# First expert matrix: both parts of the input side by side in one 512-column stream, and the one-hots of the first key on ScalarE

## The chip, the cores and the metric

The kernel runs on 1 NeuronCore of one Trainium2 chip. The metric is the device time of one execution in microseconds (us). The numbers before are three timed executions and one profiled execution of the same program.

## The reference

A hybrid layer on 256 tokens of width 2048 (16 more tokens stand ahead in its first part): retention and state-space mixing, then a product-key expert layer with 128 x 128 experts, then a last norm. What the change touches is the expert layer, for all 256 tokens at once:

```
xn   = rmsnorm(h, norm_ffn_g)                       # 256 x 2048, fp32
q    = (xn @ w_q).reshape(tokens, 8, 2, 128)        # 8 heads, two half keys
s    = einsum('thcd,hckd->thck', q, sub_keys)       # two scores of 128 keys
s1, i1 = top_k(s[:, :, 0], 16);  s2, i2 = top_k(s[:, :, 1], 16)
cand = s1[..., :, None] + s2[..., None, :]          # 256 candidates, top 16 again
eid  = i1 * 128 + i2 of the 16 chosen;  gate = softmax(top_s)
act  = gelu(einsum('td,thkd->thk', xn, exp_u[eid]))
out  = einsum('thk,thkd->td', gate * act, exp_v[eid])
```

The kernel does not gather rows. It multiplies xn by all 16384 rows of exp_u, takes the gelu, weights it by a 128 x 128 table of gates for each token, which is zero where an expert was not chosen, and multiplies by all of exp_v.

## The kernel before, in words

All weights come as 512 KB blocks of 128 x 1024 through one queue of SP (`Stream.load`, L90). A block is two *pieces* of 128 x 512. For each piece ScalarE copies the raw fp32 weights to the fp32r tile `wh` (L100), VectorE subtracts to get the rest `wl` (L101), and TensorE multiplies in three terms: high by high, low by high, high by low. The list of pieces is the program's clock: `Stream.run` goes from piece to piece, splits the piece two ahead, lets the side work that is due issue its instructions, and then issues the piece's matmuls. All orders are fixed when the program is built, and each engine works in that order.

Side work is written as generators. `yield wait, dve, act` asks for a rest of so many pieces and announces so much work on VectorE and ScalarE. `Stream.due` gives each piece a credit of 0.70 on VectorE and 0.80 on ScalarE (`SPARE`). Work that isn't urgent is put off by a piece when a credit that it wants is not above zero; a debt is carried into the next piece.

The expert layer has these stages, in the order of the pieces. In the first the input is h times the weights of the norm, not yet divided by its root mean square: `Q.xgh` and `Q.xgl`, 16 chunks of 128 x 256 each (`scaled`, L819 and L822). The reciprocal root, spread over a tile of 128 x 256, is `Q.rb` (`norm`, L835).

- Queries: 16 products of 4 pieces (`query`). From `norm` on the side work `topk` picks the keys on VectorE, some 146 pieces' worth of its credit, into `Q.i1`, `Q.i2` and the gates.
- First expert matrix ("the U stage"): 128 units of 4 pieces (`product`, L207 to L209, with 16 chunks of three matmuls of 256 columns each). After a unit VectorE multiplies the sums by `Q.rb` (L1030), and ScalarE takes the gelu (L1036, and L1038 for tokens whose gates are there already). While units run, the side work `gates` builds the gate table token by token: GpSimd makes the one-hots of the first key (L985), VectorE two weighted ones of the second key (L987), and one matmul of 256 columns makes the table (L1001). Each token asks for 0.26 on VectorE, and at most one token is taken in a piece. After four tokens `into_z` copies one half on ScalarE (L1016, asking for 0.7) and a piece later adds on VectorE (L1021, L1023, asking for 0.7) and multiplies on GpSimd (L1025, L1041). All gates have to be there before the last stage.
- Second expert matrix ("the V stage"): 128 x 4 pieces, matmuls of 512 columns (L1069 to L1071).

SP issues all loads of weights. The table `Q.iota`, which the one-hots are compared with, is loaded when the U stage opens (`u_open`, L961); `u_open` also gives back the memory of `h2p`.

Of the kernel before, what the change touches and what calls it, by code (L numbers as in the profile page):

```python
# [12 lines left out]
OP = mybir.AluOpType  # L13
# [114 lines left out]
def build(ctx, tc, a):  # L128
# [61 lines left out]
    def product(srcs, moving, done, hook=None, count=None):  # L190


        nk = 8 * len(srcs)
        box = {}

        def piece(k0):
            def f(h, lo):
                if count:
                    st.need(lambda: count() >= k0 + 4)
                mh, ml = moving()  # L200
                if k0 == 0:
                    box["p"] = P.psa.tile([128, T], F32, name="acc")
                p = box["p"][:, :mh.shape[-1]]
                for k in range(4):
                    s = slice(k * 128, k * 128 + 128)
                    kk = k0 + k
                    pe.matmul(p, h[:, s], mh[:, kk], start=kk == 0, stop=False)  # L207
                    pe.matmul(p, h[:, s], ml[:, kk], start=False, stop=False)  # L208
                    pe.matmul(p, lo[:, s], mh[:, kk], start=False, stop=kk == nk - 1)  # L209
                if k0 + 4 == nk:  # L210
                    st.spawn(done(p), 1, True)
            return f

        st.queue += [(srcs[i // 2], piece(4 * i), hook if i == 0 else None) for i in range(2 * len(srcs))]
# [568 lines left out]
    def resid_open():  # L783
        closed("gated", "xn")
        w = opened("bconst")
        Q.rb = w.tile([128, S], F32, name="rb")
        w = opened("xg")
        Q.xgh = w.tile([128, NK, S], F32R, name="xgh")
        Q.xgl = w.tile([128, NK, S], F32R, name="xgl")
        w = opened("h2p")  # L790
        Q.h2 = w.tile([128, 2, D], F32, name="h2")
        Q.ss = w.tile([128, 2, 4], F32, name="ss")
        nc.sync.dma_start(Q.h2, a["xt"])
        Q.h2d = P.dram.tile([128, 2, D], F32, name="h2d")
# [31 lines left out]
    def norm():  # L826
        yield 6
        sq = P.bconst.tile([128, 2], F32, name="sq")
        vec.tensor_reduce(sq, Q.ss, axis=AX.X, op=OP.add)
        Q.rt = P.bconst.tile([128, 2], F32, name="rt")  # L830
        rsqrt(Q.rt, sq, 1.0 / D, EPS)
        yield 3
        ps = P.psm.tile([128, 512], F32, name="mix")
        yield from rows(ps[:, :S], Q.rt, P.h2p.tile([128, 512], F32, name="junk")[:, :S])
        act.activation(Q.rb, ps[:, :S], AF.Copy)  # L835
        st.spawn(topk(), 1)

    def query_open():
        closed("mhl", "mwork", "merged")
# [43 lines left out]
    def topk():  # L883
# [53 lines left out]
        for i in range(3):  # L937
# [5 lines left out]
            tps.append(t)  # L943
            yield 1
        Q.i1, Q.i2, g = tps
        gh = P.slots.tile([128, S], F32R, name="gh")
        act.activation(gh, g, AF.Copy)
        vec.tensor_sub(g, g, gh.bitcast(F32))
# [6 lines left out]


    def u_open():
        closed("h2p")
        w = opened("bwork", 2)
        Q.iota = w.tile([128, 128], F32, name="iota", bufs=1)  # L960
        nc.sync.dma_start(Q.iota, a["iota"])  # L961
        opened("slots")
        opened("psg", 2, space=PSUM)
        w = opened("zap")
        Q.za = w.tile([128, NE - ZB, S], F32, name="za")
        Q.nblk = 0
        Q.ntok = 0
# [11 lines left out]
    def gates():  # L979
        NB = 4  # L980

        def hot(t):
            tt = slice(t, t + 1)
            o = P.ohp.tile([128, 3, 128], F32R, name="o", bufs=3)
            pool.tensor_scalar(o[:, 0], Q.iota, Q.i1[:, tt], None, op0=OP.is_equal)  # L985
            for i in range(2):
                vec.tensor_scalar(o[:, 1 + i], Q.iota, Q.i2[:, tt], Q.gg[i][:, tt], op0=OP.is_equal, op1=OP.mult)  # L987
            return o

        os = []  # L990
        for t in range(2):
            yield 1, 0.26
            os.append(hot(t))
        for t in range(S):
            yield 1, 0.26
            if t + 2 < S:
                os.append(hot(t + 2))
            if t % NB == 0:
                ps = P.psg.tile([128, NB, 2, 128], F32, name="g")
            o = os.pop(0)  # L1000
            pe.matmul(ps[:, t % NB].rearrange("p a b -> p (a b)"), o[:, 0], o[:, 1:].rearrange("p a b -> p (a b)"),  # L1001
                      start=True, stop=True)
            if t % NB == NB - 1:
                st.spawn(into_z(ps, t + 1 - NB, t + 1), 1, False, (0, 0.7))
        while Q.ntok < S:
            yield 1
        yield 1
        closed("ohp")
        opened("wp", 2, side="right")
        Q.w = {}  # L1010
        for i in range(2):
            st.spawn(split_w(i), i + 1)
# [14 lines left out]
    def unit(i):  # L1027
        def done(p):
            t = P.bwork.tile([128, S], F32, name="ut", bufs=2)
            vec.tensor_mul(t, p, Q.rb)  # L1030
            yield 1, 0, 0.45
            n = Q.ntok
            Q.nblk = i + 1
# [160 lines left out]
            q = st.queue[-8:]  # L1194
            st.queue[-8:] = q[:2] + q[4:6] + q[2:4] + q[6:]
    for i in range(NE):
        product([a["pu"][i, 0], a["pu"][i, 1]], lambda: (Q.xgh, Q.xgl), unit(i), u_open if i == 0 else None)
    for i in range(NE):
        for q in range(4):
            hook = {(0, 0): v_open, (0, 3): v_open3, (NE - ZB + 3, 0): fin_open}.get((i, q))  # L1200
# [179 lines left out]
```

## Time and profile before

| what | value |
|---|---|
| median of 3 timed runs | 3375.70 us (3375.68 to 3375.73) |
| profiled execution: its time | 3375.47 us |
| profiled execution: span of the core | 3373.7 us |
| TensorE matmul busy | 3352.7 us, 99% |
| VectorE, ScalarE, GpSimd busy | 2339.9, 1742.1, 634.8 us |

The span is what the trace covers; some 1.8 us of the execution's time lie around it. The duration that the trace gives to a matmul runs from its start to its modelled end, and matmuls overlap, so what a matmul costs is read from the spacing of the starts: the number of matmuls in a stretch that has no gap. The same holds for the other engines, where an instruction can begin before the one ahead of it has ended.

### The profile page before, as it was taken

How to read it: one execution, taken by the hardware profiler on the slowest of the kernel's cores; microseconds unless marked ns; L12 is line 12 of the kernel's file. 1: busy time of each engine (PE TensorE's matmuls, PEld its weight loads, DVE VectorE, ACT ScalarE, POOL GpSimd, SP SyncE). 2: the span in 40 equal slices, each digit the busy share in tenths (PEclk: the TensorE clock that was granted, in tenths of full speed). 3: DMA queues.
4: the chain of work that ended last, by engine and by line, in shares of the span. 5: the costliest groups of instructions: out<-in, count | busy, mean ns of one | idle time of the engine just before them, and what ended most of it. 6: DMA issues, size and time to landing. Idle time of an engine off the chain costs nothing.

```text
span 3373.7 us, 60928 instructions
## 1 busy us (share of the span) xinstructions
PE 3352.7 (99%) x22638; PEld 3101.6 (92%) x22638; DVE 2339.9 (69%) x4521; ACT 1742.1 (52%) x3148; POOL 634.8 (19%) x726
## 2 busy tenths in 40 slices
PE   9999999999999999999999999999999999999998
PEld 9999999888899999988889999999999988888886
DVE  7555555555578878865556899899999655555555
ACT  5444444444455555554455555555555555555555
POOL 1100110000023323310000111356778200000000
PEclk9999999999999999999999999999999999999999
DMA  6555555566655555556666565555555666666665
GB/s 202 159 168 164 170 167 164 173 196 205 188 175 177 176 180 182 181 172 189 188 214 211 175 188 186 178 177 176 176 176 176 187 194 193 194 194 194 218 207 162
DMA packets 174249, 619.81 MB, mean 184 GB/s; under 512 B 20320, under 2 KB 22240, under 8 KB 173696
## 3 DMA queue, kind: packets, MB, share of 16 engines
q1 hardware_dynamic: 169728, 602.16, 57.8%
q0 software_dynamic: 3648, 12.72, 1.3%
q8 instruction: 178, 2.92, 0.4%
q14 instruction: 119, 0.97, 0.1%
q10 hardware_dynamic: 576, 1.05, 0.1%
HBM read 611.52 MB, written 4.33 MB: 183 GB/s over the span
## 4 chain that ended last, share of the span: by engine, by line
PE 56%; ACT 0%; DVE 0%; issue 0%; POOL 0%; POOLq 0%; ACTq 0%
PE acc L209 8%; PE acc L208 8%; PE acc L207 8%; PE y L1069 7%; PE y L1070 7%; PE y L1071 7%; PE acc L235 3%; PE acc L236 3%; PE acc L237 3%; PE g L1001 1%; PE mix L469 0%; PE mix L863 0%; DVE wl L101 0%; ACT junk L1122 0%; ACT wh L100 0%
## 5 line engine op out<-in xcount | busy, mean ns | idle before, releaser
L101 DVE TENSOR_TENSOR wl<-raw,wh 128x512 fp32r<-128x512 f32 x2244 | 1631.9, 732 | 977.3 <-ACT wh L100 764.8
L100 ACT ACTIVATE wh<-raw 128x512 fp32r<-128x512 f32 x2244 | 1409.1, 630 | 1299.5 <-PE acc L208 664.6
L207 PE MATMUL acc<-xh,wh 128*128 128x272 f32 (+1 forms) x2640 | 768.3, 291 | 0.0
L209 PE MATMUL acc<-xh,wl 128*128 128x272 f32 (+1 forms) x2640 | 753.7, 286 | 0.6 <-DVE wl L101 0.6
L208 PE MATMUL acc<-xl,wh 128*128 128x272 f32 (+1 forms) x2640 | 751.1, 285 | 0.0
L209 PE MATMUL acc<-xgh,wl 128*128 128x256 f32 x2304 | 644.6, 280 | 0.0
L207 PE MATMUL acc<-xgh,wh 128*128 128x256 f32 x2304 | 643.9, 279 | 0.0
L208 PE MATMUL acc<-xgl,wh 128*128 128x256 f32 x2304 | 643.8, 279 | 0.0
L207 PEld LDWEIGHTS acc<-xh,wh 128*128 128x128 f32 x2640 | 497.5, 188 | 3.9 <-issue 1.2
L209 PEld LDWEIGHTS acc<-xh,wl 128*128 128x128 f32 x2640 | 497.4, 188 | 1.0 <-DVE wl L101 1.0
L208 PEld LDWEIGHTS acc<-xl,wh 128*128 128x128 f32 x2640 | 497.4, 188 | 0.7
L208 PEld LDWEIGHTS acc<-xgl,wh 128*128 128x128 f32 x2304 | 432.8, 188 | 0.1
L209 PEld LDWEIGHTS acc<-xgh,wl 128*128 128x128 f32 x2304 | 432.3, 188 | 0.0
L207 PEld LDWEIGHTS acc<-xgh,wh 128*128 128x128 f32 x2304 | 432.1, 188 | 0.1
L1069 PE MATMUL y<-wh,wzh 128*128 128x512 f32 x1024 | 398.5, 389 | 0.0
L1070 PE MATMUL y<-wl,wzh 128*128 128x512 f32 x1024 | 398.5, 389 | 0.0
L1071 PE MATMUL y<-wh,wzl 128*128 128x512 f32 x1024 | 398.5, 389 | 0.0
L1071 PEld LDWEIGHTS y<-wh,wzl 128*128 128x128 f32 x1024 | 192.2, 188 | 39.9
L1069 PEld LDWEIGHTS y<-wh,wzh 128*128 128x128 f32 x1024 | 192.2, 188 | 39.9
L1070 PEld LDWEIGHTS y<-wl,wzh 128*128 128x128 f32 x1024 | 192.2, 188 | 39.8
L985 POOL TENSOR_SCALAR o<-iota,tp 128x128 fp32r<-128x128 f32 x256 | 220.1, 868 | 22.4 <-PE g L1001 18.3
L235 PE MATMUL acc<-wh,gh 128*128 128x512 f32 x512 | 199.7, 390 | 0.0
(316 smaller groups left out, 3837.8 us busy)
## 6 DMA issues: line engine op xcount, KB each, us to landing
raw<-in_win SPq DMA_DIRECT2D x353, 512.0 KB, 3.7
raw<-in_pu SPq DMA_DIRECT2D x256, 512.0 KB, 3.6
raw<-in_pv SPq DMA_DIRECT2D x256, 512.0 KB, 4.3
raw<-in_wro SPq DMA_DIRECT2D x64, 512.0 KB, 4.1
raw<-in_wso SPq DMA_DIRECT2D x64, 512.0 KB, 4.1
raw<-in_wga SPq DMA_DIRECT2D x32, 512.0 KB, 3.8
raw<-in_wgs SPq DMA_DIRECT2D x32, 512.0 KB, 4.3
raw<-in_wout SPq DMA_DIRECT2D x32, 512.0 KB, 4.3
```

Of the source, the lines that this page charges most:

```text
L100: self.nc.scalar.activation(h, r, AF.Copy)
L101: self.nc.vector.tensor_sub(lo, r, h.bitcast(F32))
L207: pe.matmul(p, h[:, s], mh[:, kk], start=kk == 0, stop=False)
L208: pe.matmul(p, h[:, s], ml[:, kk], start=False, stop=False)
L209: pe.matmul(p, lo[:, s], mh[:, kk], start=False, stop=kk == nk - 1)
L235: pe.matmul(p, sh[:, k, t], wh, start=k == 0, stop=False)
L236: pe.matmul(p, sl[:, k, t], wh, start=False, stop=False)
L237: pe.matmul(p, sh[:, k, t], wl, start=False, stop=k == nk - 1)
L985: pool.tensor_scalar(o[:, 0], Q.iota, Q.i1[:, tt], None, op0=OP.is_equal)
L1069: pe.matmul(y, wh[:, s], h, start=i == 0, stop=False)
L1070: pe.matmul(y, wh[:, s], lo, start=False, stop=False)
L1071: pe.matmul(y, wl[:, s], h, start=False, stop=i == NE - 1)
```

## The change

A new function `product_cat` takes the place of `product` in the U stage alone. The two parts of the input, `xu[:, k, 0]` (high) and `xu[:, k, 1]` (low), lie side by side. One matmul streams both as 512 columns against `wh`, and a second streams the 256 high ones against `wl`, into the first half of the same sums. After a unit ScalarE copies the second half and VectorE adds the first. A new side work `normed` makes `xu` beforehand, with the norm multiplied in: 16 chunks, each with a sum on GpSimd, a product and a difference on VectorE and a copy on ScalarE. The one-hots of the first key are made on ScalarE as relu(1 - |iota - i1|). Each token now asks for 0.44 on ScalarE too, and every eighth token is taken in the same piece as the one ahead of it. The load of `iota` is issued earlier, when the residual opens, and the tiles get other places.

```diff
+    def product_cat(srcs, moving, done, hook=None):
...
+                if k0 == 0:
+                    box["p"] = P.psa.tile([128, 512], F32, name="acc")
+                p = box["p"]
+                for k in range(4):
+                    s = slice(k * 128, k * 128 + 128)
+                    kk = k0 + k
+                    pe.matmul(p, h[:, s], m[:, kk].rearrange("p i t -> p (i t)"), start=kk == 0, stop=False)
+                    pe.matmul(p[:, :S], lo[:, s], m[:, kk, 0], start=False, stop=kk == nk - 1)
...
         w = opened("bconst")
         Q.rb = w.tile([128, S], F32, name="rb")
+        Q.iota = w.tile([128, 128], F32, name="iota")
+        nc.sync.dma_start(Q.iota, a["iota"])
+        w.tile([128, 48], F32, name="pad")
+        Q.xu = opened("xu").tile([128, NK, 2, S], F32R, name="xu")
         w = opened("xg")
+        w.tile([128, 16], F32, name="pad")
...
         st.spawn(topk(), 1)
+        st.spawn(normed(), 2)
+
+    def normed():
+
+        x = {}
+        for k in range(NK + 1):
+            yield 2, 1.1, 0.33
+            if k < NK:
+                x[k] = t = P.h2p.tile([128, S], F32, name="xn", bufs=2)
+                pool.tensor_add(t, Q.xgh[:, k].bitcast(F32), Q.xgl[:, k].bitcast(F32))
+                vec.tensor_mul(t, t, Q.rb)
+                act.activation(Q.xu[:, k, 0], t, AF.Copy)
+            if k:
+                vec.tensor_sub(Q.xu[:, k - 1, 1], x.pop(k - 1), Q.xu[:, k - 1, 0].bitcast(F32))
...
         Q.i1, Q.i2, g = tps
+        vec.tensor_scalar(Q.i1, Q.i1, -1.0, None, op0=OP.mult)
...
     def u_open():
-        closed("h2p")
-        w = opened("bwork", 2)
-        Q.iota = w.tile([128, 128], F32, name="iota", bufs=1)
-        nc.sync.dma_start(Q.iota, a["iota"])
+        closed("h2p", "xg")
+        opened("bwork", 2)
...
             o = P.ohp.tile([128, 3, 128], F32R, name="o", bufs=3)
-            pool.tensor_scalar(o[:, 0], Q.iota, Q.i1[:, tt], None, op0=OP.is_equal)
+
+            away = P.ohp.tile([128, 128], F32, name="away")
+            act.activation(away, Q.iota, AF.Abs, bias=Q.i1[:, tt])
+            act.activation(o[:, 0], away, AF.Relu, bias=ones[:, :1], scale=-1.0)
...
         for t in range(2):
-            yield 1, 0.26
+            yield 1, 0.26, 0.44
             os.append(hot(t))
         for t in range(S):
-            yield 1, 0.26
+            if t % 8:
+                yield 1, 0.26, 0.44
...
             t = P.bwork.tile([128, S], F32, name="ut", bufs=2)
-            vec.tensor_mul(t, p, Q.rb)
+            act.activation(t, p[:, S:], AF.Copy)
+            vec.tensor_add(t, p[:, :S], t)
...
-        product([a["pu"][i, 0], a["pu"][i, 1]], lambda: (Q.xgh, Q.xgl), unit(i), u_open if i == 0 else None)
+        product_cat([a["pu"][i, 0], a["pu"][i, 1]], lambda: Q.xu, unit(i), u_open if i == 0 else None)
```

## Rows read from the trace of the kernel before

**Rows 1.** The page's parts 1 and 2: busy time of each engine with its share of the span, and the granted TensorE clock in 40 slices.

```profile
PE 3352.7 (99%) x22638; PEld 3101.6 (92%) x22638; DVE 2339.9 (69%) x4521; ACT 1742.1 (52%) x3148; POOL 634.8 (19%) x726
...
PEclk9999999999999999999999999999999999999999
```

**Rows 2.** Busy time of each engine by stretches (us from the span's start): length, then busy us and number of instructions of PE, PEld, DVE, ACT, POOL, the granted clock, the DMA share and GB/s. In order: queries; U stage before the gates; the same without its edges; the gates; a late part of the gates; V stage.

```profile
1813.00:1913.00 100.00, 100.00 (x853) 99.95 (x852) 72.94 (x196) 53.77 (x103) 9.91 (x16) 1.00 0.60 188
1913.00:2140.00 227.00, 227.00 (x1930) 227.00 (x1929) 205.37 (x580) 122.73 (x209) 33.50 (x50) 1.00 0.60 186
1920.00:2130.00 210.00, 210.00 (x1786) 210.00 (x1785) 192.01 (x546) 110.08 (x189) 29.73 (x45) 1.00 0.60 187
2152.00:2631.00 479.00, 479.00 (x4074) 478.75 (x4073) 459.36 (x1069) 268.19 (x540) 335.76 (x420) 1.00 0.57 176
...
2450.00:2550.00 100.00, 100.00 (x853) 100.00 (x852) 98.93 (x217) 56.31 (x113) 77.61 (x97) 1.00 0.57 174
...
2700.00:3300.00 600.00, 600.00 (x2649) 496.87 (x2648) 342.74 (x552) 312.62 (x551) 0.00 (x0) 1.00 0.66 199
```

**Rows 3.** Timeline of TensorE in the U stage: start in us, duration in us, engine, line, operation.

```profile
2035.06 0.28 PE L208 MATMUL acc<-xgl,wh 128*128 128x256 f32 x1
2035.17 0.28 PE L209 MATMUL acc<-xgh,wl 128*128 128x256 f32 x1
2035.29 0.28 PE L207 MATMUL acc<-xgh,wh 128*128 128x256 f32 x1
```

**Rows 4.** The same timeline in the V stage.

```profile
2900.15 0.39 PE L1071 MATMUL y<-wh,wzl 128*128 128x512 f32 x1
2900.38 0.39 PE L1069 MATMUL y<-wh,wzh 128*128 128x512 f32 x1
```

**Rows 5.** The gates' matmuls: number, duration (min/median/max ns), first and last start.

```profile
L1001 PE MATMUL g<-o x256: 279/279/386, 2152.2 to 2631.1; 128*128 128x256 f32 x128
```

**Rows 6.** Groups of ScalarE's instructions in the stretch of the gates, 2152 to 2631 us: number, then busy us and mean ns of one, then idle time ahead of them and what ended it.

```profile
L100 ACT ACTIVATE wh<-raw 128x512 fp32r<-128x512 f32 x318 | 201.0, 632 | 198.3 <-PE acc L208 169.2 <-ACT ut L1038 19.8 <-ACT g L1016 6.4
L1016 ACT ACTIVATE g<-g 128x512 f32<-128x512 f32 x63 | 36.6, 580 | 0.0
L1038 ACT ACTIVATE ut<-ut 128x4 f32<-128x4 f32 (+39 forms) x79 | 23.2, 294 | 0.0
L1036 ACT ACTIVATE za<-ut 128x252 f32<-128x252 f32 (+36 forms) x46 | 16.5, 359 | 5.7 <-DVE ut L1030 5.7
L1036 ACT ACTIVATE zb<-ut 128x108 f32<-128x108 f32 (+26 forms) x34 | 8.5, 251 | 7.2 <-DVE ut L1030 6.7
```

**Rows 7.** Single operations of ScalarE elsewhere, duration as min/median/max ns: an Exp of 128 x 128; copies of 128 x 256 with a scale read from a 128 x 1 tile (L759) and without (L1049); a copy of 128 x 256 out of the sums (L854); the table loads ahead of a gelu.

```profile
L927 ACT ACTIVATE sl<-sl x2: 310/311/312, 1985.7 to 2133.8; 128x128 f32<-128x128 f32 x2
...
L759 ACT ACTIVATE gh<-y,gss x32: 492/497/505, 1024.8 to 1485.0; 128x256 fp32r<-128x256 f32 x32
...
L1049 ACT ACTIVATE wzh<-za x88: 401/417/418, 2636.4 to 3131.6; 128x256 fp32r<-128x256 f32 x88
...
L854 ACT ACTIVATE qt<-acc x16: 384/385/385, 1820.5 to 1909.2; 128x256 f32<-128x256 f32 x16
...
L1036 ACT ACT_TABLE_LOAD x3: 1283/1283/1283, 1916.7 to 2136.8; - x3
```

**Rows 8.** Timeline of ScalarE at two places: an Abs (L509) and the Exp (L510) that reads its result; and a gelu and a second one that doesn't depend on it, with the next copy of weights.

```profile
773.31 0.43 ACT L509 ACTIVATE xs<-xs 64x272 f32<-64x272 f32 x1
773.78 0.43 ACT L510 ACTIVATE xs<-xs 64x272 f32<-64x272 f32 x1
...
2305.39 0.35 ACT L1036 ACTIVATE za<-ut 128x176 f32<-128x176 f32 x1 [0.59 <-DVE ut L1030]
2305.65 0.25 ACT L1038 ACTIVATE ut<-ut 128x80 f32<-128x80 f32 x1
2305.81 0.62 ACT L100 ACTIVATE wh<-raw 128x512 fp32r<-128x512 f32 x1
```

**Rows 9.** Groups of VectorE's instructions in the stretch of the gates, 2152 to 2631 us (columns as in Rows 6).

```profile
L101 DVE TENSOR_TENSOR wl<-raw,wh 128x512 fp32r<-128x512 f32 x319 | 244.7, 767 | 12.8 <-ACT wh L100 9.4
L987 DVE TENSOR_SCALAR o<-iota,tp,gh 128x128 fp32r<-128x128 f32 x254 | 108.6, 428 | 0.0
L987 DVE TENSOR_SCALAR o<-iota,tp,tp 128x128 fp32r<-128x128 f32 x254 | 90.2, 355 | 0.0
L1030 DVE TENSOR_TENSOR ut<-acc,rb 128x256 f32<-128x256 f32 x80 | 33.5, 419 | 7.1 <-PE acc L209 5.9
L1021 DVE TENSOR_TENSOR g<-g 128x172 f32<-128x172 f32 (+62 forms) x63 | 30.9, 490 | 0.0
```

**Rows 10.** The same groups of VectorE in the V stage, 2700 to 3300 us, where GpSimd does nothing.

```profile
L101 DVE TENSOR_TENSOR wl<-raw,wh 128x512 fp32r<-128x512 f32 x442 | 306.4, 693 | 257.9 <-ACT wh L100 257.9
```

**Rows 11.** Groups of GpSimd's instructions in the stretch of the gates (columns as in Rows 6).

```profile
L985 POOL TENSOR_SCALAR o<-iota,tp 128x128 fp32r<-128x128 f32 x253 | 217.6, 868 | 18.7 <-PE g L1001 18.3
L1025 POOL TENSOR_TENSOR za<-g,za 128x352 f32<-128x352 f32 (+36 forms) x63 | 63.1, 1002 | 122.9 <-DVE g L1021 75.0 <-ACT ut L1038 17.4 <-ACT wh L100 16.7
```

**Rows 12.** Timeline of SP's queue where the U stage opens: the load of iota and the next loads of weights.

```profile
1908.03 0.43 SPq L961 DMA_DIRECT2D iota<-in_iota  x1
1910.82 24.45 SPq L90 DMA_DIRECT2D raw<-in_pu  x9
```

More of the change, by code (lines that the diff above doesn't have):

```diff
@@ L209, in f, with piece @@
                     pe.matmul(p, lo[:, s], mh[:, kk], start=False, stop=kk == nk - 1)
+                if k0 + 4 == nk:
+                    st.spawn(done(p), 1, True)
+            return f
+        st.queue += [(srcs[i // 2], piece(4 * i), hook if i == 0 else None) for i in range(2 * len(srcs))]
+    def product_cat(srcs, moving, done, hook=None):
+        nk = 8 * len(srcs)
+        box = {}
+        def piece(k0):
+            def f(h, lo):
+                m = moving()
+                if k0 == 0:
[6 more added lines that the diff above has]
+                    pe.matmul(p[:, :S], lo[:, s], m[:, kk, 0], start=False, stop=kk == nk - 1)
                 if k0 + 4 == nk:
```

## The prediction

> **What bounds the kernel now.** I read the page's first two parts, then the busy times by stretches, then the timelines of TensorE, and last the groups of the other engines where the change puts work. TensorE is busy 99% of the span, at full granted clock in every slice [rows 1]: what it saves is saved, unless another engine comes to hold it up. Durations don't price a matmul, because they overlap: one of 256 columns lasts 0.28 us, but the next starts 0.12 us later [rows 3]. The spacing comes from counts: before the gates, 1786 matmuls in 210.0 us without a gap, 117.6 ns each; in the V stage, 2649 of 512 columns in 600.0 us, 226.5 ns each [rows 2, 4]. So 256 further columns cost 108.9 ns, and each matmul costs 8.7 ns whatever its width. This fixed part is what there is to gain.
>
> In the U stage no other engine holds TensorE up: all three stretches of it have TensorE busy to the last 0.1 us [rows 2]. But VectorE has little left: 98.9 of 100 us late in the gates. ScalarE has room, 268 of 479 us [rows 2].
>
> **The matmuls.** Before, a chunk takes three matmuls of 256 columns, 3 x 117.6 = 352.7 ns. After, one of 512 and one of 256: 226.5 + 117.6 = 344.1 ns. The columns, 768, stay the same, and only one fixed part goes. With 128 x 16 = 2048 chunks that is 2048 x 8.66 ns = **17.7 us**. No row shows the two widths in turn. Bounds: if the fixed part were really paid per 256 columns, a 512 here would cost 235.2 ns and the gain is nothing; if the short matmul behind a long one lost its fixed part too, the gain is 35.4 us. I take 17.7, since both widths show their own spacing in long runs.
>
> [...]
>
> **How fast the gates run.** This sets how dense the added work is. Before, 256 tokens ran from 2152.2 to 2631.1 us [rows 5], over 318 pieces [rows 6]: five pieces for four tokens. The credit says why: the second half of `into_z` takes the whole 0.70 of a piece, and a token waits. With 0.44 on ScalarE for each token, next to 0.7 for four tokens and 0.45 for a unit, two tokens in four would be put off in some groups; with each eighth token riding along, I work the rule through to eight tokens in nine pieces, 288 pieces in all. On TensorE these last 288 x 4 x 344.1 ns + 256 x 117.6 ns = 426.5 us.
>
> **ScalarE in the gates.** Abs and Relu of 128 x 128 with a per-partition bias: an Exp of that size takes 0.31 us, and a per-partition operand adds 497 - 417 = 80 ns [rows 7], so 0.39 us each. The Relu reads the Abs and starts 0.03 us after its end, as Exp did behind Abs; a successor that depends on nothing starts 0.09 us before the end [rows 8]. That makes 0.39 + 0.03 + 0.39 - 0.09 = 0.72 us for a token, 184 us for 256. The copies of half the sums: 72 units x (0.385 - 0.09) = 21 us [rows 7]. From the 268 us of before go 30 pieces x 0.632 = 19 us [rows 6]. Sum: 268 - 19 + 184 + 21 = 454 us. That still counts the old instructions at full length, as before, when ScalarE mostly ran dry behind each. If its queue never runs dry, some 400 of them begin 0.09 us earlier, and the sum is 418 us. So 418 to 454 us against 426.5 us of TensorE. A queue this full is near the lower end, and I take 418: it just fits, at 98%.
>
> **VectorE in the gates.** 459 us busy [rows 2], less 30 pieces x 0.767 and 8 units x 0.42 [rows 9]: 433 us. GpSimd's one-hots, 217.6 of its 336 us [rows 2, 11], are gone, and with them some contention: a subtraction lasts 767 ns here and 693 ns where GpSimd is still [rows 9, 10], a one-hot beside it 428 and 355 ns. All of that gone would give 433 - 288 x 0.074 - 256 x 0.073 = 393 us. GpSimd's products (L1025) stay, so neither end holds. I take the middle, 413 us, which fits. Late it is tighter. A piece of twelve matmuls took 12 x 117.6 ns = 1.411 us and takes 4 x 344.1 ns = 1.376 us after. Four tokens took 5 x 1.411 + 4 x 0.118 = 7.53 us, 98.9% of it busy, 7.44 us. After, 4.5 pieces with four gate matmuls give 6.66 us, and VectorE wants 7.44 - 0.43 = 7.01 at worst, 6.4 at best. At worst that is 0.35 us for each of the last 24 groups (some 180 us of before), 8 us.
>
> Both engines near 98%, each waiting on the other (the difference needs ScalarE's copy; the gelu needs VectorE's sum), will hold TensorE up now and then. The first copy of a unit also can't start before TensorE has ended the unit, so ScalarE can't work ahead over that point, and clumps of tokens have to fit in the lead that is left: of the three pieces (4.1 us) from there to the next weights' due time, the copy, a token and the two halves of a split (0.63 and 0.69 us) take 2.4, which leaves some 1.7 us. **I book 5 us** of stalls, out of 0 to 28 us (the upper end is 454 - 426.5).
>
> **What I book at nothing.** `normed`: 17 steps of two pieces are 34 of the 64 query pieces, and begin some 18 pieces in. VectorE has 27 us to spare in 100 us there, ScalarE 46 and GpSimd 90 [rows 2]; the 32 operations on VectorE at 0.42 us [rows 9] come to 13 us. If the cover were gone, these 13 us would show. They do use up credit: 17 x 1.1 / 0.70 = 27 pieces by which the key search ends later. The first token came some (2152 - 1913) / 1.411 = 169 pieces into the U stage; now 196, and 196 + 288 = 484 against 487 before, of 512. So the V stage doesn't wait. The sums: ScalarE's copy makes their release some 0.4 us later, and each buffer is wanted again only a unit, 5.5 us, later. SP: the load of iota leaves the U stage's start, where it cost the queue 2.8 us [rows 12] with no gap on TensorE, and stands beside the load of h, which waits for the same memory; the weights are six pieces ahead there. The sign of i1 is one short operation. The V stage has the same instructions.
>
> **Table loads.** Gelu cost a load of 1.28 us only three times, though 63 copies (L1016) ran among the gelus [rows 6, 7]. That Abs and Relu can stand there without a load, no row shows. [...] If it were wrong, two loads for each of 72 units are 185 us.
>
> **The sum.** The profiled execution took 3375.47 us, 0.2 us under the median of the runs, so I use the one for the other. 3375.5 - 17.7 + 5 = **3363 us**.
>
> **Rivals.**
>
> 1. ScalarE becomes the bound of the gates, in its own queue. Each wait of a gelu or of a copy out of the sums lets the queue run dry, and the sum is nearer 454 us. For it: nothing in the trace shows ScalarE over 70% for long, and its instructions wait on two engines. Against it: back-to-back starts are 0.09 us early wherever the next one is ready [rows 8]. At the upper end: 3357.8 + 28 = 3386 us, slower. It decides from 444 us on, where the stall eats all 17.7 us. A part of it, with 11 to 24 us of stall, ends at 3369 to 3382, no difference to be told.
> 2. The change does not give what it says: the columns stay the same, and the fixed part belongs to columns and not to the matmul. Then 3375.5 plus 0 to 5, 3376 to 3380 us. Against it: the 8.7 ns stand in two long stretches [rows 2].
> 3. More than one fixed part goes: 3375.5 - 35.4 + 5 = 3345 us. The row for the short matmul comes from short ones alone; behind a long one there is more time to change the weights.
> 4. The table loads: 185 us more on ScalarE, well over 3500 us.
>
> **How the numbers follow.** My forecast, 3358 to 3368 us: 0.60. Better, down to 3345: 0.08. Part of the first rival: 0.14. No gain: 0.06. The first rival in full, and the table loads (0.02): 0.12. What a measurement can tell from no change is about 0.2%, 6.8 us: faster is under 3369 us and slower over 3382 us. So faster 0.60 + 0.08 = 0.68, same 0.14 + 0.06 = 0.20, slower 0.12. The range goes from 3350, halfway to the third rival, to 3384, near the end of the first; that leaves out some 0.06 below and 0.10 above.
>
> **What would show it.** Right: in the U stage before the gates a 512-column matmul followed by the next start after 0.227 us, the short one after 0.118, and a chunk in 0.344; in the gates 256 tokens over about 288 pieces, ScalarE over 90% busy, and idle time of TensorE under 10 us in total, ended by `wh`, `wl` or the one-hots; a subtraction on VectorE nearer 0.70 than 0.77 us; no further table loads; the V stage at 226.5 ns. Wrong: a chunk of 0.353 us (rival 2) or 0.335 (rival 3); ScalarE busy all through the gates with TensorE idle ahead of `wh` by over 18 us (rival 1); or a gap where the V stage opens, if the gates end later than I worked out.

## The result, and the profile after

The changed kernel takes 3409.84 us (median of 4 runs, 3409.74 to 3410.13) against 3375.69 us for the kernel before on the same chip: a ratio of 1.0102, interval 1.0091 to 1.0114. It is 34 us slower, where 3363 us were forecast and 3384 was the end of the range.

Where the time went is read first from where the V stage begins. The line of its first matmul, of before and then of after (number, durations, first and last start):

```profile
L1069 PE MATMUL y<-wh,wzh x1024: 388/389/398, 2663.7 to 3359.4; 128*128 128x512 f32 x171
```

```profile
L231 PE MATMUL acc<-xu,wh x607: 390/391/392, 1919.8 to 2129.9; 128*128 128x512 f32 x152
...
L1046 PE MATMUL g<-o x256: 278/280/417, 2174.1 to 2649.1; 128*128 128x256 f32 x128
...
L1115 PE MATMUL y<-wh,wzh x1024: 388/389/395, 2697.7 to 3393.4; 128*128 128x512 f32 x171
```

The V stage opens 34.0 us later and lasts as long as before. By the starts of its matmuls, from the first to the last, the U stage takes 788.74 us against 754.63; the queries take 98.37 against 98.02. So all of it is in the U stage. In front of the gates that stage is faster: 607 chunks from 1919.8 to 2129.9 us are 346.7 ns each, against 353.3 counted in the same way in before (352.7 by the counts of [rows 2], which take in matmuls that only reach into the stretch). The gates lose it. They last 475.0 us where 426.5 were worked out (before: 478.9 over more pieces [rows 5]); TensorE isn't busy all through them any more, as it was in [rows 2]. Busy time by stretches of after, columns as there:

```profile
1920.00:2130.00 210.00, 210.00 (x1214) 185.48 (x1213) 193.28 (x556) 123.01 (x231) 38.23 (x47) 1.00 0.57 190
...
2174.00:2649.00 475.00, 446.49 (x2553) 386.48 (x2552) 426.83 (x1029) 417.16 (x1073) 120.88 (x160) 0.99 0.48 159
...
2540.00:2543.50 3.50, 1.74 (x10) 1.19 (x9) 3.08 (x7) 2.29 (x7) 1.39 (x3) 1.00 0.46 149
2543.60:2547.00 3.40, 3.40 (x13) 2.92 (x13) 2.49 (x9) 3.05 (x8) 0.00 (x0) 0.50 0.35 119
```

ScalarE's 417.16 us are what was forecast (418), but over 475 us. It isn't full: 58 us of the stretch are idle. What each engine waited for there (total us, times, longest), TensorE, ScalarE, VectorE:

```profile
PE g L1046 <- DVE o L1031: 11.2, 17, 1.4
PE g L1046 <- ACT o L1029: 8.2, 8, 1.2
PE g L1046 <- ACT ut L1084: 5.6, 7, 0.9
PE g L1046 <- ACT away L1028: 2.7, 3, 1.3
...
ACT ut L1075 <- PE acc L232: 25.7, 47, 1.5
ACT za L1082 <- DVE ut L1076: 12.7, 10, 1.6
ACT zb L1082 <- DVE ut L1076: 9.3, 8, 1.5
...
DVE wl L101 <- ACT wh L100: 44.9, 84, 0.8
DVE ut L1076 <- ACT ut L1075: 3.2, 12, 0.6
```

TensorE waits for one-hots, nearly never for weights. ScalarE stands 25.7 us at the copy out of the sums, which needs the unit's last matmul, and 22 us at the gelu, which needs VectorE's sum. VectorE in turn stands 44.9 us for ScalarE's `wh` and 3.2 for the copy; with its 426.83 us of work that is the whole stretch, and it is idle for nothing else. In what follows, *stalls* are the sum, from the first gate matmul to the end of the U stage, of what the starts of two successive matmuls lie further apart than 231 ns (behind 512 columns) or 118 ns, where this is over 40 ns. Before had 0.4 us of them, after has 44.0: 31.1 between two gate matmuls that follow each other directly (31 times: the eighth tokens, which ride along), 5.5 ahead of other gate matmuls, the rest behind them, of which some 5 are three stretches of 3.4 us at the granted clock 0.50. Here is one of the 31, in the timelines of TensorE, ScalarE and VectorE:

```profile
2301.12 0.36 PE L1046 MATMUL g<-o 128*128 128x256 f32 x1 [0.15 <-DVE o L1031]
2302.63 0.39 PE L1046 MATMUL g<-o 128*128 128x256 f32 x1 [1.15 <-ACT o L1029]
...
2299.10 0.36 ACT L1075 ACTIVATE ut<-acc 128x256 f32<-128x256 f32 x1
2299.36 0.62 ACT L100 ACTIVATE wh<-raw 128x512 fp32r<-128x512 f32 x1
2301.34 0.36 ACT L1082 ACTIVATE za<-ut 128x188 f32<-128x188 f32 x1 [1.36 <-DVE ut L1076]
2301.61 0.24 ACT L1084 ACTIVATE ut<-ut 128x68 f32<-128x68 f32 x1
2301.76 0.39 ACT L1028 ACTIVATE away<-iota,tp 128x128 f32<-128x128 f32 x1
2302.18 0.40 ACT L1029 ACTIVATE o<-away,ones 128x128 fp32r<-128x128 f32 x1
2302.49 0.61 ACT L100 ACTIVATE wh<-raw 128x512 fp32r<-128x512 f32 x1
...
2299.31 1.15 DVE L101 TENSOR_TENSOR wl<-raw,wh 128x512 fp32r<-128x512 f32 x1
2300.39 0.34 DVE L1031 TENSOR_SCALAR o<-iota,tp,gh 128x128 fp32r<-128x128 f32 x1
2300.64 0.34 DVE L1031 TENSOR_SCALAR o<-iota,tp,tp 128x128 fp32r<-128x128 f32 x1
2300.90 0.41 DVE L1076 TENSOR_TENSOR ut<-acc,ut 128x256 f32<-128x256 f32 x1
2301.23 0.68 DVE L101 TENSOR_TENSOR wl<-raw,wh 128x512 fp32r<-128x512 f32 x1
2301.83 0.34 DVE L1031 TENSOR_SCALAR o<-iota,tp,gh 128x128 fp32r<-128x128 f32 x1
2302.09 0.35 DVE L1031 TENSOR_SCALAR o<-iota,tp,tp 128x128 fp32r<-128x128 f32 x1
2303.13 0.69 DVE L101 TENSOR_TENSOR wl<-raw,wh 128x512 fp32r<-128x512 f32 x1 [0.70 <-ACT wh L100]
```

Read it backwards. The gate matmul at 2302.63 needs ScalarE's Relu, which ends at 2302.58, and VectorE's second one-hot, which ends at 2302.44. The Relu and its Abs stand on ScalarE behind the gelu, and the gelu waits 1.36 us for VectorE's sum, which stands behind a difference of weights and two one-hots. ScalarE had nothing to do meanwhile. VectorE worked without a gap, from the sum to the next difference and to the one-hots that TensorE waits for. And behind ScalarE's late one-hot stands the next `wh`, at 2302.49, for which VectorE then waits 0.70 us. Each engine hands its delay to the other.

Which operand is late is seen by comparing, for all gate matmuls that start over 40 ns late, the ends of the two one-hots. There are 49 of them, with 36.6 us. At 44 (30.5 us) VectorE's came last, most often 0.145 us before the matmul's start, and ScalarE's had been there for 1.3 us (the median). At the other 5, the one above among them, ScalarE's came last, but VectorE's only 0.01 to 0.15 us before it. (The list above names ScalarE more often, but for `ut` and `away`, which the matmul doesn't read, and in part for the one-hot of a later token, which ended just then.) So TensorE waits for VectorE's one-hots. What ScalarE's waits do to them goes by way of `wh` and the copy. In the 4 us before 27 of the 44, though, VectorE was idle for less than 0.2 us: there it had fallen behind earlier, or has too much to do around a riding token. This trace doesn't tell which; the runs below say more.

### The profile page after: what moved, and what is told of

Same layout as the page of the kernel before. It is cut to its first block, busy times and chain, and to the rows that moved or that the text cites. A ratio compares the mean times of both kernels' runs of the same rounds, so it can differ in the third digit from the quotient of the medians.

```text
span 3408.0 us, 57217 instructions
## 1 busy us (share of the span) xinstructions
PE 3357.2 (99%) x20590; PEld 3009.1 (88%) x20590; DVE 2341.9 (69%) x4553; ACT 1932.6 (57%) x3796; POOL 441.7 (13%) x482
## 4 chain that ended last, share of the span: by engine, by line
PE 51%; ACT 2%; DVE 2%; issue 1%; POOL 0%; DVEq 0%; POOLq 0%; ACTq 0%
PE acc L231 11%; PE y L1116 7%; PE y L1117 7%; PE y L1115 7%; PE acc L232 6%; PE acc L258 3%; PE acc L259 3%; PE acc L260 3%; PE acc L209 1%; PE acc L208 1%; PE acc L207 1%; DVE wl L101 1%; PE g L1046 1%; DVE o L1031 1%; ACT wh L100 1%
## 5 line engine op out<-in xcount | busy, mean ns | idle before, releaser
L231 PE MATMUL acc<-xu,wh 128*128 128x512 f32 x2048 | 728.0, 396 | 0.0
L232 PE MATMUL acc<-xu,wl 128*128 128x256 f32 x2048 | 575.3, 281 | 0.0
L231 PEld LDWEIGHTS acc<-xu,wh 128*128 128x128 f32 x2048 | 386.7, 189 | 78.0
L232 PEld LDWEIGHTS acc<-xu,wl 128*128 128x128 f32 x2048 | 389.3, 190 | 0.0
L259 PE MATMUL acc<-wh,gl 128*128 128x512 f32 x512 | 199.5, 390 | 0.0
L260 PE MATMUL acc<-wl,gh 128*128 128x512 f32 x512 | 199.5, 390 | 0.0
L258 PEld LDWEIGHTS acc<-wh,gh 128*128 128x128 f32 x512 | 96.2, 188 | 20.1 <-issue 0.2
```

The source lines that it names most:

```text
L231: pe.matmul(p, h[:, s], m[:, kk].rearrange("p i t -> p (i t)"), start=kk == 0, stop=False)
L232: pe.matmul(p[:, :S], lo[:, s], m[:, kk, 0], start=False, stop=kk == nk - 1)
L258: pe.matmul(p, sh[:, k, t], wh, start=k == 0, stop=False)
L259: pe.matmul(p, sl[:, k, t], wh, start=False, stop=False)
```

## The experiments

Four causes were to be told apart. The *lead* (theory 1): the one-hots, by the riding tokens, come too late, since the planner issues them only one piece ahead of their matmul. *Throughput* (theory 2): ScalarE has too much to do. The *hop* (theory 3): the gelu's wait for VectorE's sum holds ScalarE's queue. And, from the first runs on, *W*: the two waits at the head of ScalarE's queue, the copy's for the end of the unit and the gelu's for the sum, which hold up all that is queued behind them, the one-hots and the `wh` that VectorE needs. The 52 us of stalls in the first expectation are another count than the 44.0 here. The times are medians of 3 rounds against before on the same chip; ratios with their intervals.

**The lead alone.** One-hots made three tokens ahead, with four buffers (and, for the room, Abs and Relu in one tile and `rb` in another pool).

```diff
-            o = P.ohp.tile([128, 3, 128], F32R, name="o", bufs=3)
+            o = P.ohp.tile([128, 3, 128], F32R, name="o", bufs=4)
...
-        for t in range(2):
+        for t in range(3):
...
-            if t + 2 < S:
-                os.append(hot(t + 2))
+            if t + 3 < S:
+                os.append(hot(t + 3))
```

> The changed kernel, but each token's one-hots are issued three tokens ahead of their matmul instead of two, with four buffers in place of three. To make room, rb lies in memory that is given back when the U stage opens, and Abs is written in place of the one-hot. The pace of the gates stays eight tokens in nine pieces. Theory 1 (lead): the token that rides along is used one piece after its one-hots are issued, the others two or three, and TensorE waits for that one; with three ahead each has two or more, so nearly all of the 52 us of stalls go: 3357 to 3364 us. Theory 2 (throughput): ScalarE and VectorE can't keep the pace of eight tokens in nine pieces; a longer lead changes nothing after the first tokens: 3404 to 3411 us. Theory 3 (hop): ScalarE loses its time where a gelu waits for VectorE's sum; that wait stays, and a part of the stalls goes: 3375 to 3395 us.

3394.14 us, 1.0058 (1.0041 to 1.0075); stalls 27.8; in the range of theory 3 alone. A longer lead gives back 16 of 34 us and no more: ScalarE still waits 32.6 us at the gelu. The lead is longer for VectorE's one-hots too, since both engines' are issued together.

**No riding along.** Every token asks for its rest (318 pieces as before; `normed` announces 0.8 instead of 1.1). Once with the one-hots on ScalarE, once on GpSimd as before.

```diff
-            if t % 8:
-                yield 1, 0.26, 0.44
+            yield 1, 0.26, 0.44
```

> The changed kernel, but no token rides along: at most one in a piece, four in five pieces by the credit, 318 pieces for the gates. So that they end in time, normed announces 0.8 instead of 1.1 on VectorE. ScalarE still makes the one-hots. Theory 1 (lead): each token has two or three pieces of lead, 3357 to 3364 us. Theory 2 (throughput): the same work now has 318 x 1.38 + 30 = 468 us, nearly as long as the 475 us that it took with stalls: stalls of 5 to 15 us are left, 3363 to 3373 us. Theory 3 (hop): the wait for VectorE's sum stays, 3370 to 3390 us.

> As no_double, but GpSimd makes the one-hots of the first key as before the change. This leaves of the change the matmuls of 512 columns, the split sum and the norm made beforehand. All theories: the gain on the matmuls alone, 17 to 18 us less than before, 3357 to 3361 us. If it is more, the fixed part was mis-sized; if it lies at 3365 or above, VectorE with GpSimd's contention can't follow the shorter pieces.

3388.61 us, 1.004 (1.0026 to 1.0054), stalls 18.9; and 3373.21 us, 0.9995 (0.9985 to 1.0004), stalls 5.0. Riding along is a part, and with it gone the one-hots on ScalarE still cost 15 us. From 2174 to 2640 us VectorE waits 38.5 us for `wh` with them on ScalarE, and 8.3 with them on GpSimd. All theories had 3357 to 3361 us for the second run, and all missed it. Its U stage is only 6.35 us shorter than before's, stalls included, and its queries are 4.4 us longer: at 0.8 the steps of `normed` come denser, TensorE waits 1.27 us for `wh` at 1875.6 us, and 1.6 us later the clock is at 0.50 for 3.4 us.

**The two waits.** The copy is issued a piece later, the gelu two pieces behind the sum; each alone, and both.

```diff
         def done(p):
+            yield 1
             t = P.bwork.tile([128, S], F32, name="ut", bufs=2)
             act.activation(t, p[:, S:], AF.Copy)
             vec.tensor_add(t, p[:, :S], t)
-            yield 1, 0, 0.45
+            yield 2, 0, 0.45
```

Only the second edit:

> The changed kernel, but the gelu comes two pieces after the sum instead of one, so that VectorE's sum is there when ScalarE comes to it. Theory 3 (hop): the 22 us in which ScalarE waits for the sum go, and most of the stalls with them: 3362 to 3380 us. Theory 1 (lead): the token that rides along still has one piece: 3395 to 3410 us, a part better since its piece is often that of the gelu. Theory 2 (throughput): 3400 to 3410 us.

3393.16 us, 1.0054 (1.0037 to 1.007), stalls 27.8: between the ranges of theories 3 and 1. Only the first:

> The copy of the half sums is issued one piece later than in the change; the gelu stays one piece behind the sum (so it moves one piece as well). It separates the two waits of ScalarE's queue. If the wait for the end of the unit's products at the copy is what matters (25.7 us in the change's trace against 22 at the gelu, and the late gelu alone gave 17 us of 34), the stalls fall from 44 to 15 to 20 us and the time is 3379 to 3386 us. If both waits are one loop that has to be broken in both places, it stays near the late gelu alone: 3390 to 3397. If the copy is all of it, 3373 to 3378.

3399.0 us, 1.007 (1.0053 to 1.0087), stalls 34.3. Both:

> The changed kernel, but the copy of half the sums comes a piece later, and the gelu two pieces after that. So ScalarE finds the unit ended and VectorE's sum made when it comes to them. Theory W (waits at the head of ScalarE's queue): in the gates of the changed kernel ScalarE was busy 417 us of 475 and stood 48 us before a copy or a gelu; with those waits gone its 417 us fit into 287 pieces of 1.39 us and 30 us of gate matmuls, 429 us, and nearly all stalls go: 3363 to 3374 us. Theory 2 in a milder form (two engines near full hold each other up wherever the waits stand): no better than with the gelu alone moved, 3385 to 3394 us.

3375.31 us, 1.0001 (0.9991 to 1.001), stalls 9.4: 1 us above the range of W, and 10 below that of theory 2. What ScalarE waited for in the gates, in the run with the late gelu, with the late copy, and with both:

```profile
ACT ut L1075 <- PE acc L232: 30.9, 55, 2.0
```

```profile
ACT za L1083 <- DVE ut L1077: 18.5, 19, 1.6
ACT zb L1083 <- DVE ut L1077: 12.9, 12, 1.6
```

```profile
ACT wh L100 <- PE acc L231: 14.8, 34, 0.9
```

With one wait moved, the other grows to 31 us: from 25.7 at the copy, from 22 at the gelu. With both moved neither is left; ScalarE now stands at `wh`, for a buffer that TensorE hasn't read yet, which means that it is ahead. VectorE's wait for `wh` falls with it, here from 2190 to 2630 us, where it was 41.4 us in the change:

```profile
DVE wl L101 <- ACT wh L100: 18.0, 41, 0.7
```

The moved waits gave 17 and 11 us singly and 34 together: it is one loop, which has to be opened in both places. The late copy alone ends 2 us above what its expectation had for that case.

**Throughput.** Every second one-hot of the first key, the riding ones among them, on GpSimd.

```diff
+            if t % 2:
+                away = P.ohp.tile([128, 128], F32, name="away")
+                act.activation(away, Q.iota, AF.Abs, bias=Q.i1[:, tt], scale=-1.0)
+                act.activation(o[:, 0], away, AF.Relu, bias=ones[:, :1], scale=-1.0)
+            else:
+                pool.tensor_scalar(o[:, 0], Q.iota, Q.i1[:, tt], None, op0=OP.is_equal)
```

> The changed kernel, but GpSimd makes the first key's one-hot of every second token, those that ride along among them; the sign of i1 goes into ScalarE's scale. Takes 92 us from ScalarE, and gives GpSimd 110. Theory W and theory 2 both: ScalarE is at 325 of 429 us and can wait at its head without harm, 3363 to 3371 us. If the short lead of the token that rides along is a cause by itself, its stalls of some 0.4 us stay: 3372 to 3380 us.

3390.28 us, 1.0044 (1.0028 to 1.0061), stalls 24.9. Busy time of the gates, and ScalarE's waits:

```profile
2174.00:2640.00 466.00, 449.34 (x2614) 391.33 (x2613) 437.10 (x1044) 344.56 (x834) 233.75 (x290) 1.00 0.48 167
```

```profile
ACT ut L1077 <- PE acc L232: 68.8, 66, 2.1
ACT wh L100 <- PE acc L231: 19.1, 48, 0.9
ACT za L1084 <- DVE ut L1078: 11.9, 14, 1.5
ACT zb L1084 <- DVE ut L1078: 11.1, 13, 1.4
```

ScalarE is 74% busy, with over 110 us of waits, and TensorE still stalls for 25. So less work on ScalarE gives back 20 of the 34 us, but a full ScalarE is not the whole cause. The time freed is spent waiting at the copy, 68.8 us where it was 25.7. No theory had this: W too gave 3363 to 3371 us, as it took a wait at the head for harmless where ScalarE has time. What TensorE waited for shows no one-hot of ScalarE any more:

```profile
PE g L1048 <- DVE o L1033: 12.4, 21, 1.0
PE g L1048 <- POOL o L1031: 4.0, 6, 0.9
```

The GpSimd line is a cost of this run's own, at six late gate matmuls.

**The one-hots without the new matmuls.** The kernel before, with Abs and Relu on ScalarE in place of GpSimd's comparison, and nothing else.

```diff
-            pool.tensor_scalar(o[:, 0], Q.iota, Q.i1[:, tt], None, op0=OP.is_equal)
+            away = P.ohp.tile([128, 128], F32, name="away")
+            act.activation(away, Q.iota, AF.Abs, bias=Q.i1[:, tt], scale=-1.0)
+            act.activation(o[:, 0], away, AF.Relu, bias=ones[:, :1], scale=-1.0)
```

> The kernel before, with ScalarE in place of GpSimd for the one-hots of the first key and nothing else: matmuls of 256 columns, no copy of half the sums, four tokens in five pieces. ScalarE then has some 268 + 184 us less what overlaps, about 420 of 479 us, and one wait a unit, that of the gelu for VectorE. Theory W: it fits, 3374 to 3380 us. If one-hots on ScalarE by themselves hold TensorE up: 3384 to 3395 us.

3384.51 us, 1.0028 (1.0018 to 1.0038), stalls 9.6. This kernel has no copy and no riding, only the gelu's wait:

```profile
ACT zb L1038 <- DVE ut L1032: 30.3, 26, 1.9
ACT za L1038 <- DVE ut L1032: 18.2, 22, 1.9
```

Before, the same wait was 12.4 us (5.7 + 6.7 [rows 6]). W had 3374 to 3380 us, and missed. VectorE's wait for `wh`, 9.4 us in all the gates of before [rows 9], is now this, from 2190 to 2630 us alone:

```profile
DVE wl L101 <- ACT wh L100: 30.3, 61, 0.7
```

At all 19 late gate matmuls (8.0 us) VectorE's one-hot came last. So the one-hots on ScalarE delay `wh`, and by it VectorE, without the copy and without riding along.

**The matmuls in groups.** Four of 512 columns, then four of 256, in each piece.

```diff
                 for k in range(4):
...
                     pe.matmul(p, h[:, s], m[:, kk].rearrange("p i t -> p (i t)"), start=kk == 0, stop=False)
+                for k in range(4):
+                    s = slice(k * 128, k * 128 + 128)
+                    kk = k0 + k
                     pe.matmul(p[:, :S], lo[:, s], m[:, kk, 0], start=False, stop=kk == nk - 1)
```

> The changed kernel, but a piece issues its four matmuls of 512 columns first and then its four of 256. The 512 ones came every 230.6 ns in the U stage instead of 226.5 as in the V stage. Theory a (turns): the 4 ns come from a change of widths, and three of four go: 226.6 ns among the 512, some 6 us less, 3400 to 3406 us. Theory b (place): they come from where xu lies or how it is read, the spacing stays at 230 ns, 3406 to 3412 us.

3413.42 us, 1.0112 (1.0095 to 1.0129). In front of the gates two 512-column matmuls in a row start 234.1 ns apart, two short ones 118.5; in turn it was 230.0 and 116.7. So it is not the change of widths that keeps the 512 from its 226.5 ns. The run is slower than either theory had it.

**Both waits and the lead.** The edits of the first experiment and of both waits together.

> Copy one piece later, gelu two pieces after the sum, and one-hots made three tokens ahead. With the two waits moved, 9.4 us of stalls were left, 8.2 of them between two gate matmuls, at the token that rides along. If these come from the one-hot that is issued only one piece ahead, a longer lead takes most: stalls 2 to 4 us, time 3368 to 3371 us. If they come from ScalarE being at 94 per cent, the lead changes nothing: 3374 to 3377.

3368.24 us, 0.9979 (0.997 to 0.9989), stalls 1.6. It beats both kernels. The gates (2174 to 2630 us) and the start of the V stage:

```profile
2174.00:2630.00 456.00, 455.50 (x2686) 400.60 (x2685) 437.74 (x1056) 427.48 (x1103) 125.19 (x165) 1.00 0.53 176
...
L1115 PE MATMUL y<-wh,wzh x1024: 389/389/395, 2656.0 to 3351.6; 128*128 128x512 f32 x171
```

ScalarE is 94% busy and VectorE 96%, both more than in the change (88 and 90%), and TensorE is busy all but 0.5 us. That is the plainest answer to theory 2, for both engines. No run took work from VectorE, so what its load adds was not tried.

**GpSimd's one-hots with both waits moved.** Riding along stays, at a lead of two tokens.

```diff
-            away = P.ohp.tile([128, 128], F32, name="away")
-            act.activation(away, Q.iota, AF.Abs, bias=Q.i1[:, tt])
-            act.activation(o[:, 0], away, AF.Relu, bias=ones[:, :1], scale=-1.0)
+            pool.tensor_scalar(o[:, 0], Q.iota, Q.i1[:, tt], None, op0=OP.is_equal)
```

> Copy one piece later and gelu two pieces after the sum, as before, but GpSimd makes the one-hots of the first key again; the tokens still ride along. ScalarE then has some 200 us less to do in the gates. If what is left of the loss once the waits are moved is ScalarE's load, 9.4 us of stalls fall to 3 or less: 3366 to 3370 us. If the riding tokens need a faster maker than GpSimd with two tokens of lead, TensorE waits for GpSimd at the riding tokens: 3374 to 3382.

3377.98 us, 1.0008 (0.9998 to 1.0017), stalls 12.2, 10.7 of them at riding tokens. TensorE's waits and the busy time of the gates:

```profile
PE g L1043 <- POOL o L1026: 7.3, 10, 1.3
```

```profile
2174.00:2614.00 440.00, 431.74 (x2534) 378.39 (x2534) 425.62 (x1026) 258.37 (x559) 329.09 (x408) 1.00 0.50 171
```

With ScalarE at 59% the riding tokens still come late, most of them now by GpSimd's one-hot (10 of 15): the short lead costs some 10 us whoever makes the one-hot.

**Why a 512-column matmul takes 230 ns.** Three runs on the matmul term: both waits moved, with the products 96 bytes lower in SBUF; and the best version with every matmul streaming the first chunk, and with the two sides of the long matmul swapped (these two run once each; they leave out the sums that their expectations name).

```diff
-        w.tile([128, 48], F32, name="pad")
+        w.tile([128, 24], F32, name="pad")
...
-        w.tile([128, 16], F32, name="pad")
+        w.tile([128, 40], F32, name="pad")
```
```diff
-                    pe.matmul(p, h[:, s], m[:, kk].rearrange("p i t -> p (i t)"), start=kk == 0, stop=False)
-                    pe.matmul(p[:, :S], lo[:, s], m[:, kk, 0], start=False, stop=kk == nk - 1)
+                    pe.matmul(p, h[:, s], m[:, 0].rearrange("p i t -> p (i t)"), start=kk == 0, stop=False)
+                    pe.matmul(p[:, :S], lo[:, s], m[:, 0, 0], start=False, stop=kk == nk - 1)
```
```diff
-                    pe.matmul(p, h[:, s], m[:, kk].rearrange("p i t -> p (i t)"), start=kk == 0, stop=False)
+                    pe.matmul(p, m[:, kk, 0, 0:128], h, start=kk == 0, stop=False)
```

> Copy one piece later and gelu two pieces after the sum, and the norm's products lie 96 bytes lower in SBUF; nothing else. It asks of the 230.6 ns that a 512-column matmul takes from them, against 226.5 in the last stage, whether they come from where the moving data begins. If so, the spacing falls to 226.5 to 228 ns and the first expert stage by 5 to 8 us: 3367 to 3371 us. If the place has no part in it, 230 to 231 ns and 3375 us within 2.

> The best version, with every matmul of the first expert matrix streaming the products of the first chunk (the sum over the other chunks is left out and that of the first is made sixteen times instead). If the 230.6 ns come from walking through 32 KB of products, the spacing falls to 226 to 228 ns; if not, it stays at 230 to 231.

> The best version, with the two sides of the 512-column matmul swapped: 128 columns of the products are the weights and the 512 columns of the staged high part stream, as in the last stage (the first expert matrix's sums are left out and replaced by others of the same shape). If what streams sets the spacing, it falls from 230.6 to 226 to 227 ns; if it is something of the stage (its accumulation, or that every second matmul is shorter), it stays at 230 to 231.

3373.48 us, 0.9995 (0.9985 to 1.0005); 3368.39 us; 3367.91 us. In the stretch 1920 to 2130 us each starts 607 chunks in 210.1 us, 346.7 ns, as the change does; here the swapped one:

```profile
L231 PE MATMUL acc<-wh,xu x607: 390/391/392, 1919.7 to 2129.8; 128*128 128x512 f32 x152
```

So the 4 ns come neither from the walk through the products nor from what streams. The 96 bytes shift the two spacings against each other, 229.2 and 117.5 ns for 230.0 and 116.7, and leave the chunk as it is. Within the gates they do a little: a chunk takes 347.4 ns where it took 348.6 with both waits moved, and the U stage is 1.3 us shorter. What else the U stage has that the V stage hasn't, its neighbour of 256 columns or its long accumulation into one set of sums, wasn't told apart.

## Why the prediction was wrong

**The step that failed: "I book 5 us of stalls", and under it "it just fits, at 98%" of ScalarE and "which fits" of VectorE.** There were 44.0 us. ScalarE's numbers were right: 417 us (418 forecast), 287 pieces (288), the first token at piece 190 (196), Abs and Relu 391 and 403 ns (0.39 us each), and no further table load, as `L1082` has three loads of 1.28 us, as in [rows 7]. VectorE had 426.83 us of work, not 413. TensorE's own work in the gates is some 431 us at the spacings measured there, so VectorE had 4 us to spare, and it waited 48 for ScalarE: 427 + 48 = 475 us, as long as the gates took. Fitting by the sum, each engine by itself, was the wrong test. An engine that works its queue in order fits only if its waits at the head of that queue fit as well. ScalarE works its queue so, as the trace shows: the Abs, which needs nothing of the gelu, begins behind it at 2301.76, after the gelu's wait of 1.36 us. ScalarE's waits came to 47.7 us (25.7 + 12.7 + 9.3), and 417 + 48 = 465 of the 475 us that the gates took. I saw both waits, and priced them together by the pipelining that ScalarE would lose, 0 to 28 us. Their price is the time that the other engine needs, up to 1.6 us at each, and VectorE pays it where `wh` stands behind. With 4 us to spare it can't make up for it, and TensorE waits for VectorE's one-hots. The runs show the cause: waits moved and lead lengthened, and 1.6 us of stalls are left at a higher load of both engines. The way by `wh` and VectorE is read from the traces.

**The shorter lead** of the riding tokens was not priced at all. I used the riding tokens to count pieces, and did not ask how far ahead of its matmul a riding token's one-hots are made. By the credit rule it is one piece. With the waits in place the longer lead was worth 16 us, with the waits moved 7.1 us (3375.31 to 3368.24).

**The first rival** named the place and the direction, but as a sum: full at 454 us, 3386 at most. ScalarE's sum never came near, and 3410 us lay outside. By the runs its condition is not a busy share but whether ScalarE reaches the copy ahead of the unit's end, and the gelu ahead of the sum: with half its one-hots gone it came earlier and just waited longer at the copy, and 15 us were still lost.

**The matmul term** was right in sign, and too large. A chunk takes 346.7 ns in front of the gates (344.1 forecast) and 349.2 within them (232.8 + 116.4, by the mean spacing of the starts without the stalls), against 353.3 and 352.5 before. The forecast's 117.6 and 226.5 ns count matmuls that only reach into the stretch; from start to start they are 117.8 and 226.7. The best version's U stage is 7.8 us shorter with 1.2 us more of stalls than before, so the matmuls gave 9.0 us, not 17.7, which was not the cause of the miss. "Both widths show their own spacing in long runs" did not hold: the V stage's spacing did not carry over. The second and the third rival are both out: the gain is neither nothing nor double.

**VectorE** was taken too low: 413 us forecast, 426.83 measured. A difference of weights still lasts 762 ns (218.6 us for 287), where it was 767 [rows 9], though GpSimd fell from 336 to 121 us. The slowness does go with GpSimd, but with its products and not with its one-hots, which were all that the change took away. In the change, 188 differences with no GpSimd instruction beside them last 685 ns (695 at most), and the 99 beside a product 907 (up to 1403). Before, those beside one-hots alone last 690 ns, and those beside a product 878.

**Booked at nothing, and nearly right:** `normed` (0.35 us in the queries), the load of iota, the V stage.

**The account:** 44.0 - 0.4 us of stalls, less some 9 us of matmuls, and 0.35 us in the queries make 35 us; the span grew by 34.3.

## What to carry to other kernels

When work moves to an engine with room, look at what stands at the head of its queue, not only at its busy share: each instruction there that waits for another engine delays all that is queued behind it (the gelu's 1.36 us above held up a one-hot and the next `wh`). If a third engine with little to spare needs some of that, as VectorE needed `wh` (44.9 us of waits), the delay goes on to what the bound engine wants next, and the bound engine pays. So compare the ends of all operands of a late instruction before naming the one that held it up. Issue such an instruction late enough that its operand is there (a piece or two cost nothing here: with both waits moved and the lead longer, TensorE was busy all but 0.5 us of the gates), in all places of the loop at once, since one wait moved alone comes back at the next. And when steps are merged to issue fewer of them, work out how far ahead each operand is then made.

## What the runs showed of the hardware

Some stalls of TensorE here cost more than themselves. After the stall that ends at 2542.66 (1.73 us between two starts) the granted clock goes from 1.00 to 0.50 for 3.4 us, from 2543.6 on (shown above: 13 matmuls there):

```profile
2540.93 0.36 PE L1046 MATMUL g<-o 128*128 128x256 f32 x1 [0.39 <-DVE o L1031]
2542.66 0.35 PE L1046 MATMUL g<-o 128*128 128x256 f32 x1 [1.38 <-DVE o L1031]
...
2543.43 0.28 PE L232 MATMUL acc<-xu,wl 128*128 128x256 f32 x1
2543.55 0.57 PE L231 MATMUL acc<-xu,wh 128*128 128x512 f32 x1
2543.91 0.42 PE L232 MATMUL acc<-xu,wl 128*128 128x256 f32 x1
```

Each of the three stretches at 0.50 costs 1.6 us, by what its starts lie further apart than 230 and 117 ns. The stall that ends at 2302.63 (1.51 us between two starts) had no such stretch behind it; what decides wasn't tried.

And the time of a matmul was not set by its width alone: of 512 columns it took 226.7 ns in the V stage (of the change as of before), 230.0 in turn with short ones, 232.8 beside the gates and 234.1 in groups of four, from start to start.

What slowed VectorE here was what GpSimd did beside it, not how long GpSimd was busy: a difference of weights took 685 ns with GpSimd still, 690 beside its one-hots in the kernel before, and 907 beside its products; over the gates its mean went from 767 to 762 ns while GpSimd's busy time fell from 336 to 121 us.
